# Two orders changed in a transformer trunk on one core: the spread of the row norms, and the keys of the memory attention

## The chip, the core and the metric

The kernel runs on one core of one Trainium2 chip. The core has five engines, each with its own in-order queue: TensorE (PE, matmul and weight load), VectorE (DVE), ScalarE (ACT), GpSimd (POOL) and SyncE (SP, which issues the DMAs here). They wait for each other through semaphores. The metric is the time of one execution on the device in microseconds (us), the median of several runs.

## What is computed

Two layers of a trunk over 512 tokens of width 1024, in float32. Cut to what the change touches:

```python
def _rmsnorm(x, g):
    y = xf * lax.rsqrt(jnp.mean(xf * xf, axis=-1, keepdims=True) + EPS)
    return y * g

for layer in range(2):
    x = x + 0.5 * _swiglu(_rmsnorm(x, ffn_pre_norm), w_gu, w_down)      # gate, up: 2816 each
    h = _rmsnorm(x, mix_norm)
    x = x + (_even_mixer(h, ...) if layer % 2 == 0 else _mla_mixer(h, ...))
    x = x + _memory_cross_attention(_rmsnorm(x, xmem_norm), _rmsnorm(mem, xmem_mem_norm), ...)
    x = x + 0.5 * _swiglu(_rmsnorm(x, ffn_post_norm), w_gu, w_down)

def _memory_cross_attention(hq, hm, wq, wkv, q_g, k_g, wo):              # 4 heads of 256, 256 memory tokens
    q = _rmsnorm((hq @ wq), q_g)
    k, v = jnp.split(hm @ wkv, 2)                                        # per head: 256 columns of k, 256 of v
    k = _rmsnorm(k, k_g)
    o = softmax(q @ k.T / 16) @ v
    return o @ wo
```

## The kernel before

The residual stream lies on chip with features on partitions (`x0` to `x7`, each 128 x 512 tokens). Every product runs as three passes (lines 98, 99 and 100) over operands split into a high and a low part: `hh` and `hl` for the activations, `wh` and `wl` for the weights. A weight granule (`gran`, 128 x 1024) is loaded by SP into `wr`, its high part is cast by ACT (line 79), and its low part is subtracted (line 83) by POOL, or by DVE where `lo="dve"` is given, as in the memory's products. Three raw buffers and four split ones stand between the loads and TensorE.

A norm's gain is put into `hh` and `hl`; its root mean square is applied to the product afterwards, so that the product needs no norm to begin. The factor comes in two steps, both in `stats`. First four short matmuls (line 147; the profile shows eight, since a float32 matmul is two) sum the squares `sqs` of each token, and a chain of small DVE operations (`rsqrt`, lines 106 to 114, and the copy to `rc`, line 151) takes the inverse root. If `bc` is set, DVE then builds four diagonal tiles `dg` (line 156), four matmuls spread them over all partitions (line 160), and ACT copies the result to `rbc` (line 162). `stats` with `bc` is called in each of the four FFNs after the first pair of products, and once in `sgu`, in layer 0's mixer, after the first chunk. The FFN multiplies `pg` (gate) and `pu` (up) by `rbc` on DVE (lines 220 and 222); its products take turns in five PSUM banks. In `sgu` the chunks are scaled by `rc`, and `rbc` is read much later, in `stick`.

`memkv` computes keys and values of the memory in eight chunks `c` of 256 columns: an even chunk is a head's key, the odd one after it its value. A key's chunk goes through ACT (`tk`, and its squares into `kss`), through the `rsqrt` chain on DVE and a multiplication by the result (line 928); then the closure `fin` turns it: four transposes on TensorE (line 935), ACT for the high part (line 939) and DVE for the low part (line 940). `fin` of a key is called after the next key's product, and that of the last key after the last value's product.

The code runs under a scheduler that sets each engine's order while the program is built, by a priority that follows the order of the code; nothing is reordered on the chip. `queued()` gives a rule to it: what the block issues on TensorE comes behind the last matmul that `self.pe` names (the last of a product).

Of the kernel before, what the change touches and what calls it, by code (L numbers as in the profile page):

```python
# [26 lines left out]
class Trunk:  # L27
    """The residual stream xT lives feature-major on chip; every product runs as
    three fp32r passes over operands split exactly into a high and a low part."""

    def __init__(self, ctx, tc, a, stop=None):
# [10 lines left out]
        # PSUM: two banks stay through all phases, which start in their own banks and end in these two,  # L42
        # so that no phase's first product waits for the last one's evacuation
# [3 lines left out]
    def queued(self):  # L47
        """What the block issues on the tensor engine comes behind what it had before."""
        return self.tc.issue_after(self.pe.ins)
# [9 lines left out]
    # ---------------------------------------------------------------- pieces  # L59
    def constants(self):  # L60
# [3 lines left out]
        # the first weights ahead of x: their split takes longer  # L64
# [10 lines left out]
    def split(self, hi, lo, src, eng_hi="act", eng_lo="dve"):  # L75
        """hi = src rounded to the multiplier's width, lo = src - hi (exact)."""
        nc = self.nc
        if eng_hi == "act":
            nc.scalar.copy(out=hi, in_=src)  # L79
        else:  # L80
            nc.vector.tensor_copy(out=hi, in_=src)
        e = nc.vector if eng_lo == "dve" else nc.gpsimd
        e.tensor_tensor(out=lo, in0=src, in1=hi.bitcast(F32), op=ALU.subtract)  # L83

    def gran(self, src, kt, cols, lo="pool"):
        """A weight granule [128, kt*cols] loaded and split."""
# [15 lines left out]
    def rsqrt(self, ssq, n, scale, eps, shape=None):  # L102
        """1/sqrt(ssq*scale + eps) on [128, n] by bit estimate and three Newton steps."""
# [13 lines left out]
    def prep(self, g, f):  # L117
        """Split gain*x_f for the next norm's consumers."""
# [12 lines left out]
    def squares(self, f):  # L131
        """Add the squares of x_f to the sums of the next norm."""
# [9 lines left out]
    def stats(self, pp, tag, bufs=None, bc=False):  # L142
        """rstd of every token: rc [128, NT] by token tile, and, if bc, rbc broadcast over partitions."""
# [10 lines left out]
        dg = self.t(self.sp, [P, NT, P], "dg", bufs=1)  # L154
        for t in range(NT):
            nc.vector.tensor_scalar(out=dg[:, t, :], in0=self.ident, scalar1=self.rc[:, t:t + 1], scalar2=None,
                                    op0=ALU.mult)
        ps = self.t(pp, [P, S], tag, bufs=bufs)
        for t in range(NT):
            nc.tensor.matmul(ps[:, t * P:(t + 1) * P], lhsT=self.ones, rhs=dg[:, t, :],  # L160
                             start=(t == 0), stop=(t == NT - 1), skip_group_check=True)
# [10 lines left out]
    def out_half(self, ps, w, src, kh, first):  # L172
        """One half of the contraction of a pair of out_proj's output tiles, in steps."""
# [7 lines left out]
    def out_proj(self, pp, tag, w, src, order, g, begun=None):  # L181
        """x += src @ w by pairs of output tiles; w in granules [pair*2 + khalf] of [128, 4, 256].
        begun: accumulators that hold the first half already."""
# [15 lines left out]
    # ---------------------------------------------------------------- FFN  # L199
    def ffn(self, w_gu, w_dn, g_next, out=None):  # L200
        nc, tc = self.nc, self.tc
        with tc.tile_pool(name=self.nm("ffn"), bufs=1) as fp, \
                tc.tile_pool(name=self.nm("ffps"), bufs=5, space=bass.MemoryType.PSUM) as pp:
            H = NFF // 2
            for half in range(2):
                acts = []
                for j in range(H):
# [8 lines left out]
                    if jj == 0:  # L216
                        self.stats(pp, "st", 1, True)
                    t1 = self.t(fp, [P, S], "t1", bufs=2)
                    t2 = self.t(fp, [P, S], "t2", bufs=2)
                    nc.vector.tensor_tensor(out=t1, in0=pg, in1=self.rbc, op=ALU.mult)  # L220
                    nc.scalar.activation(out=t1, in_=t1, func=AF.Silu)
                    nc.vector.tensor_tensor(out=t2, in0=pu, in1=self.rbc, op=ALU.mult)  # L222
                    nc.vector.tensor_tensor(out=t2, in0=t2, in1=t1, op=ALU.mult)
                    ah = self.t(fp, [P, S], f"ah{j}", F32R)
                    al = self.t(fp, [P, S], f"al{j}", F32R)
                    self.split(ah, al, t2, "act", "dve")
                    acts.append((ah, al))
# [15 lines left out]
    # ---------------------------------------------------------------- token-major products  # L243
    def tok_chunk(self, pp, tag, grans):
        """h @ w for 256 columns, token-major: two banks of [128, 2, 256]."""
# [11 lines left out]
    # ---------------------------------------------------------------- layer 0's mixer  # L257
# [15 lines left out]
    def sgu(self, p, pp, v, og):  # L273
# [8 lines left out]
        # only s <= t mixes: partition s, free t  # L282
# [12 lines left out]
        for dst, c0 in ((g, 0), (u, 2)):  # L295
            for c in range(2):
                ps = self.tok_chunk(pp, "mm", [w[(c0 + c) * 2], w[(c0 + c) * 2 + 1]])
                if first:
                    self.stats(pp, "tp", 2, True)
                    first = False  # L300
                for t in range(NT):
# [31 lines left out]
    def stick(self, p, pp, v, ob, src):  # L333
        """Stick-breaking attention, scores as [key, query]: causal blocks only."""
        nc, a = self.nc, self.a
        # key block -> (unit, column of its queries j*128.. in the unit); units are one bank each
# [9 lines left out]
        # -1 where row key >= column key  # L346
# [3 lines left out]
        # far below every score where key >= query: no softplus there, and no weight  # L350
# [10 lines left out]
        def proj(qk, pr, s):  # L361
            """q or k of a pair of heads, in steps."""
# [18 lines left out]
        def filler():  # L381
            """Products that wait for nothing, between the steps of the heads: the next pairs' q and k,
            and the part of the output projection that is fed by the gate."""
# [13 lines left out]
        def scores(h):  # L397
            """z of a head and the split softplus of its causal part."""
# [25 lines left out]
        def weights(st):  # L424
            """Suffix sums of the softplus, and the weights."""
# [41 lines left out]
    # ---------------------------------------------------------------- layer 1's mixer  # L467
    def rope_tables(self, p, op):
        """cos and sin of positions * inv_freq for [token, tile, 16], reduced modulo 2 pi by an
        exact digit scheme, and multiplied into the q and k gains of the two rope halves."""  # L470
# [59 lines left out]
    def mla(self):  # L530
        nc, tc, a = self.nc, self.tc, self.a
        H = 16
        with ExitStack() as outer:
# [20 lines left out]
            # the late tiles take the space of the stage before, so that the early ones need not wait for it  # L554
# [6 lines left out]
    def lora(self, p, pp, c, n, ss, cT, lg, j0):  # L561
        """rmsnorm of the token-major c [128, NT, n], turned feature-major and split."""
# [56 lines left out]
    def mla_attn(self, p, pl, pp, cT, krr, skr, gqk, neg, tq, o):  # L619
# [7 lines left out]
        def norms(st):  # L627
            """rstd of the heads' k (0) and q (1) from their sums of squares."""
            ss = st["ss"]
            # k's sums lack the rope part, which all heads share  # L630
# [11 lines left out]
        def proj_kv(st, g, t):  # L642
            """k (nope) and v of head group g, token tile t; after the last, the norms."""
# [22 lines left out]
        def proj_q(st, g, t):  # L666
            """q of head group g, token tile t; after the last, its rope."""
# [17 lines left out]
            # rope of q with its gains, in place  # L685
# [11 lines left out]
        def turn(st, h):  # L697
            """qT, kT [96, 512] of one head, split."""
# [17 lines left out]
        # query block -> (unit, column); key block j of the transposed weights likewise  # L716
# [4 lines left out]
        def filler():  # L721
            """The projections of the next head groups, a token tile at a time."""
# [18 lines left out]
        def scores(n, qk):  # L741
            """Scores of a head by query block, and their softmax."""
# [6 lines left out]
            for u, blks in enumerate(((3,), (2, 0), (1,))):  # L749
# [6 lines left out]
                # the last key block of every query block: side by side in the bank  # L756
# [24 lines left out]
        def weights(pb, wT, units):  # L781
            """The weights by key block."""
# [330 lines left out]
```

## Time and profile before

| | |
|---|---|
| median of 3 runs | 2326.71 us (2326.22 to 2329.08) |
| span of the profiled execution | 2328.0 us, 1.3 us over the median |
| TensorE busy | 98% of the span |
| VectorE, ScalarE, GpSimd busy | 44%, 38%, 39% |
| DMA | 209 MB, 29% of the 16 engines' time |

A busy share is an average over stages. The profile also lists, for each engine, whom it waited for and how long, and it can show the instructions of a stretch in order of time with the idle time of the engine before each. The granted clock is TensorE's: 1.00 is 2.4 GHz and 0.50 is 1.2 GHz. Time counts from the span's start. The ends of matmuls are modelled and overlap; how fast they follow each other is read from their starts.

### The profile page before, as it was taken

What the parts mean: (1) busy time and instruction counts of PE and PEld (TensorE: products, weight loads), DVE (VectorE), ACT (ScalarE), POOL (GpSimd) and SP (SyncE); (2) the same over time, 40 slices, a digit from 0 to 9 for tenths busy, and PEclk for the clock granted to TensorE, in tenths of its full rate; (3) what the DMA queues carried; (4) which work ended last, traced back from release to release, by engine and by line L of the source; (5) the groups of instructions that cost most, each with busy time, mean ns of one, the idle gap of its engine ahead of it and who ended that gap; (6) DMA issues with size and microseconds to landing.
All of it is one profiled execution on the core that took longest, in us unless ns stands there. A gap on an engine that the chain in (4) does not pass through costs nothing. (4 is left out here: it accounts for less than half of the span.)

```text
span 2328.0 us, 28369 instructions
## 1 busy us (share of the span) xinstructions
PE 2274.4 (98%) x11152; PEld 1891.5 (81%) x11152; DVE 1018.2 (44%) x1830; ACT 875.1 (38%) x1448; POOL 903.4 (39%) x441
## 2 busy tenths in 40 slices
PE   7999999999999999999999999998999999999999
PEld 6888888977988788888878888897768887888887
DVE  5322433465745533133343133368886545430330
ACT  4222233355644332232332223346655443322321
POOL 4444444201242444444544444434212323445443
PEclk9999999999999999999999999999999999999999
DMA  4223323311431232332322332321103313323322
GB/s 152 92 87 113 92 82 118 92 46 47 134 110 55 83 99 81 110 100 83 108 90 83 108 100 86 99 80 57 37 19 119 127 55 91 91 79 111 100 81 92
DMA packets 67350, 208.65 MB, mean 90 GB/s; under 512 B 8592, under 2 KB 10640, under 8 KB 67216
## 3 DMA queue, kind: packets, MB, share of 16 engines
q1 hardware_dynamic: 67216, 206.83, 29.1%
q8 instruction: 88, 1.44, 0.3%
q14 instruction: 46, 0.38, 0.1%
HBM read 204.70 MB, written 2.10 MB: 89 GB/s over the span
## 5 line engine op out<-in xcount | busy, mean ns | idle before, releaser
L83 POOL TENSOR_TENSOR wl<-wr,wh 128x1024 fp32r<-128x1024 f32 (+2 forms) x382 | 850.6, 2227 | 1253.0 <-ACT wh L79 1188.8
L79 ACT CAST wh<-wr 128x1024 fp32r<-128x1024 f32 (+3 forms) x423 | 408.7, 966 | 1029.8 <-PE mm L99 540.7
L98 PE MATMUL mm<-hh,wh 128*128 128x512 f32 x1440 | 562.8, 391 | 6.6 <-ACT hh L125 6.6
L100 PE MATMUL mm<-hh,wl 128*128 128x512 f32 x1440 | 562.5, 391 | 0.9 <-POOL wl L83 0.9
L99 PE MATMUL mm<-hl,wh 128*128 128x512 f32 x1440 | 562.2, 390 | 0.5 <-DVE hl L126 0.5
L98 PEld LDWEIGHTS mm<-hh,wh 128*128 128x128 f32 x1440 | 271.5, 189 | 62.9 <-ACT hh L125 6.6
L100 PEld LDWEIGHTS mm<-hh,wl 128*128 128x128 f32 x1440 | 271.6, 189 | 57.6 <-POOL wl L83 1.3
L99 PEld LDWEIGHTS mm<-hl,wh 128*128 128x128 f32 x1440 | 271.3, 188 | 57.6 <-DVE hl L126 1.0
L98 PE MATMUL A<-ah,wh 128*128 128x512 f32 x704 | 277.4, 394 | 0.0
L100 PE MATMUL A<-ah,wl 128*128 128x512 f32 x704 | 276.0, 392 | 0.0
L99 PE MATMUL A<-al,wh 128*128 128x512 f32 x704 | 273.2, 388 | 0.0
L222 DVE TENSOR_TENSOR t<-mm,rbc 128x512 f32<-128x512 f32 x88 | 60.8, 691 | 390.5 <-PE mm L100 390.5
L234 DVE SCALAR_TENSOR_TENSOR x<-A,x 128x512 f32<-128x512 f32 x64 | 44.3, 691 | 354.3 <-PE A L100 354.3
L83 DVE TENSOR_TENSOR al<-t,ah 128x512 fp32r<-128x512 f32 x88 | 160.8, 1828 | 59.1 <-ACT ah L79 59.1
L100 PEld LDWEIGHTS A<-ah,wl 128*128 128x128 f32 x704 | 132.1, 188 | 31.0
L99 PEld LDWEIGHTS A<-al,wh 128*128 128x128 f32 x704 | 132.2, 188 | 29.6
L98 PEld LDWEIGHTS A<-ah,wh 128*128 128x128 f32 x704 | 132.3, 188 | 26.4
L220 DVE TENSOR_TENSOR t<-mm,rbc 128x512 f32<-128x512 f32 x88 | 60.9, 692 | 117.1 <-PE mm L100 110.8
L126 DVE SCALAR_TENSOR_TENSOR hl<-x,gc,hh 128x512 fp32r<-128x512 f32 x64 | 82.8, 1307 | 36.7 <-ACT hh L125 36.6
L98 PE MATMUL A<-hh,wh 128*128 128x512 f32 x224 | 91.6, 410 | 0.7 <-ACT hh L79 0.7
L99 PE MATMUL A<-hl,wh 128*128 128x512 f32 x224 | 90.0, 402 | 0.0
L100 PE MATMUL A<-hh,wl 128*128 128x512 f32 x224 | 89.8, 401 | 0.0
(322 smaller groups left out, 3260.6 us busy)
## 6 DMA issues: line engine op xcount, KB each, us to landing
wr<-in_w_gu SPq DMA_DIRECT2D x176, 512.0 KB, 3.6
wr<-in_w_dn SPq DMA_DIRECT2D x64, 384.0 KB, 3.1
wr<-in_w_dn SPq DMA_DIRECT2D x64, 320.0 KB, 2.9
wr<-in_xmem_wkv SPq DMA_DIRECT2D x32, 512.0 KB, 3.2
wr<-in_xmem_wq SPq DMA_DIRECT2D x16, 512.0 KB, 3.3
wr<-in_xmem_wo SPq DMA_DIRECT2D x16, 512.0 KB, 3.2
wr<-in_sbg_w_zv SPq DMA_DIRECT2D x12, 512.0 KB, 3.5
wr<-in_sbg_w_qk SPq DMA_DIRECT2D x8, 512.0 KB, 3.6
```

The source lines that it names most:

```text
L79: nc.scalar.copy(out=hi, in_=src)
L83: e.tensor_tensor(out=lo, in0=src, in1=hi.bitcast(F32), op=ALU.subtract)
L98: mm(out, lhsT=A[0], rhs=B[0], start=start, stop=False, skip_group_check=True)
L99: mm(out, lhsT=A[0], rhs=B[1], start=False, stop=False, skip_group_check=True)
L100: self.pe = mm(out, lhsT=A[1], rhs=B[0], start=False, stop=stop, skip_group_check=True)
L126: nc.vector.scalar_tensor_tensor(out=hl, in0=self.x[f], scalar=col, in1=hh.bitcast(F32), op0=ALU.mult, op1=ALU.subtract)
L220: nc.vector.tensor_tensor(out=t1, in0=pg, in1=self.rbc, op=ALU.mult)
L222: nc.vector.tensor_tensor(out=t2, in0=pu, in1=self.rbc, op=ALU.mult)
L234: nc.vector.scalar_tensor_tensor(out=self.x[m], in0=ps, scalar=0.5, in1=self.x[m], op0=ALU.mult, op1=ALU.add)
```

## The change

Three things are altered, and comments are taken out.

- `stats` ends with the diagonal tiles, and the four spreading matmuls with the copy to `rbc` become a function of their own, `spread`.
- In `ffn` the sums are issued right behind one product and the spread right behind the next one: behind the first and the second product in three FFNs, behind the second and the third in the first FFN of the program (`s0` is 1 there). There the gating of the first pair is written behind the second pair. In `sgu` the spread is issued behind the third chunk instead of in the second.
- In `memkv` the chunks come in the order 0, 2, 1, 4, 3, 6, 5, 7, and a key is turned when two more chunks have been issued.

```diff
     def stats(self, pp, tag, bufs=None, bc=False):
@@
-        dg = self.t(self.sp, [P, NT, P], "dg", bufs=1)
+        self.dg = self.t(self.sp, [P, NT, P], "dg", bufs=1)
         for t in range(NT):
-            nc.vector.tensor_scalar(out=dg[:, t, :], in0=self.ident, scalar1=self.rc[:, t:t + 1], scalar2=None,
+            nc.vector.tensor_scalar(out=self.dg[:, t, :], in0=self.ident, scalar1=self.rc[:, t:t + 1], scalar2=None,
                                     op0=ALU.mult)
+
+    def spread(self, pp, tag, bufs=None):
+
+        nc, dg = self.nc, self.dg
         ps = self.t(pp, [P, S], tag, bufs=bufs)
         for t in range(NT):
-            nc.tensor.matmul(ps[:, t * P:(t + 1) * P], lhsT=self.ones, rhs=dg[:, t, :],
-                             start=(t == 0), stop=(t == NT - 1), skip_group_check=True)
+            self.pe = nc.tensor.matmul(ps[:, t * P:(t + 1) * P], lhsT=self.ones, rhs=dg[:, t, :],
+                                       start=(t == 0), stop=(t == NT - 1), skip_group_check=True)
         nc.scalar.copy(out=self.rbc, in_=ps)
@@ ffn: gated() holds the lines that stood in the loop (t1, t2, ah, al)
+            s0 = 1 if self.first else 0
+            todo = []
...
-                    if jj == 0:
-                        self.stats(pp, "st", 1, True)
...
+                        n = 2 * jj + (ps is pu)
+                        if n in (s0, s0 + 1):
+                            with self.queued():
+                                self.stats(pp, "st", 1, True) if n == s0 else self.spread(pp, "st", 1)
+                    todo.append((j, pg, pu))
+                    if 2 * jj > s0 or s0 == 0:
+                        for z in todo:
+                            acts.append(gated(*z))
+                        todo = []
@@ sgu
                 if first:
                     self.stats(pp, "tp", 2, True)
                     first = False
+                elif dst is u and c == 0:
+                    with self.queued():
+                        self.spread(pp, "tp", 2)
@@ memkv
-        fin = None
-        for c in range(8):
+        fins = []
+
+        for n, c in enumerate((0, 2, 1, 4, 3, 6, 5, 7)):
...
+            while fins and fins[0][0] <= n - 2:
+                with self.queued():
+                    fins.pop(0)[1]()
             if c % 2 == 1:
...
-                if c == 7:
-                    fin()
                 continue
-            if fin is not None:
-                fin()
...
+            fins.append((n, fin))
```

TensorE's queue at the start of the second FFN, before: `mm_6537` is the second product (`pu` of the first pair), `mm_6640` the third; each has 24 matmuls.

```order
L100 MATMUL mm_6537<-hh_1144_6517,wl_6571 128x512
L147 MATMUL st_6598<-ones_105,sqs_6288 128x1 x4
L98 MATMUL mm_6640<-hh_1100_6279,wh_6644 128x512
...
L98 MATMUL mm_6640<-hh_1116_6361,wh_6644 128x512
L99 MATMUL mm_6640<-hl_1117_6362,wh_6644 128x512
L160 MATMUL st_6624<-dg_6619,ones_105 128x128 x4
L100 MATMUL mm_6640<-hh_1116_6361,wl_6645 128x512
L98 MATMUL mm_6640<-hh_1128_6434,wh_6644 128x512
```

The same place in the changed program; `mm_6536` is the first product.

```order
L100 MATMUL mm_6536<-hh_1144_6517,wl_6541 128x512
L147 MATMUL st_6568<-ones_105,sqs_6288 128x1 x4
L98 MATMUL mm_6537<-hh_1100_6279,wh_6596 128x512
...
L98 MATMUL mm_6537<-hh_1144_6517,wh_6596 128x512
L99 MATMUL mm_6537<-hl_1145_6518,wh_6596 128x512
L100 MATMUL mm_6537<-hh_1144_6517,wl_6597 128x512
L164 MATMUL st_6624<-dg_6589,ones_105 128x128 x4
L98 MATMUL mm_6640<-hh_1100_6279,wh_6644 128x512
```

The sums (`st` with `sqs`) moved one product earlier, and between them and the spread (`st` with `dg`) now stand 24 matmuls instead of 11.

TensorE's queue at the end of `memkv` in layer 0, before: `mm_5328` is the last key's chunk (`tk_5399` is made from it), `mm_5422` the last value's, of 48 matmuls each, and `A_5508` the first product of the queries.

```order
L100 MATMUL mm_5328<-wh_5361,ml_854_4813 128x256
L935 MATMUL at_5389<-ident_100,tk_5239 128x128 x2
L935 MATMUL at_5394<-ident_100,tk_5239 128x128 x2
L98 MATMUL mm_5422<-wh_5425,mh_832_4757 128x256
...
L100 MATMUL mm_5422<-wh_5455,ml_854_4813 128x256
L935 MATMUL at_5488<-ident_100,tk_5399 128x128 x2
L935 MATMUL at_5493<-ident_100,tk_5399 128x128 x2
L98 MATMUL A_5508<-hh_742_4482,wh_5511 128x512
```

The same place in the changed program: `mm_5262` is the last key's chunk (`tk_5333` is made from it), `mm_5356` and `mm_5422` are the last two values'.

```order
L100 MATMUL mm_5262<-wh_5295,ml_854_4813 128x256
L956 MATMUL at_5323<-ident_100,tk_5173 128x128 x2
L956 MATMUL at_5328<-ident_100,tk_5173 128x128 x2
L98 MATMUL mm_5356<-wh_5359,mh_832_4757 128x256
...
L100 MATMUL mm_5422<-wh_5455,ml_854_4813 128x256
L956 MATMUL at_5483<-ident_100,tk_5333 128x128 x2
L956 MATMUL at_5488<-ident_100,tk_5333 128x128 x2
L98 MATMUL A_5508<-hh_742_4482,wh_5511 128x512
```

Between the last key's chunk and its transposes now stand two chunks (96 matmuls) instead of one. SP's queue is the same in both programs.

## Rows read from the trace of the kernel before

**Rows 1.** Page, part 1: busy time, share of the span, instructions.

```profile
PE 2274.4 (98%) x11152; PEld 1891.5 (81%) x11152; DVE 1018.2 (44%) x1830; ACT 875.1 (38%) x1448; POOL 903.4 (39%) x441
```

**Rows 2.** TensorE's waits: for whom, us in total, times, longest.

```profile
PE st L160 <- DVE dg L156: 8.8, 4, 2.4
PE at L935 <- DVE tk L928: 7.8, 2, 3.9
...
PE A L98 <- ACT prk L657: 3.0, 1, 3.0
...
PE tp L160 <- DVE dg L156: 2.6, 1, 2.6
```

**Rows 3.** TensorE by stretch: length, busy, instructions, granted clock, DMA share, GB/s.

```profile
397.90:401.30 3.40, 3.40 (x18) 0.50 0.02 5
804.00:807.50 3.50, 3.02 (x11) 0.51 0.25 101
1170.50:1174.00 3.50, 3.21 (x18) 1.00 0.19 76
664.00:670.90 6.90, 5.86 (x16) 0.51 0.17 67
1834.90:1841.70 6.80, 5.71 (x16) 0.50 0.20 72
```

**Rows 4.** Timeline, last FFN: start, us, engine, line, tiles, idle before, releaser.

```profile
1963.15 0.68 DVE L140 TENSOR_TENSOR sqs<-sqs,sq 128x512 f32<-128x512 f32 x1
...
1964.62 0.39 PE L98 MATMUL mm<-hh,wh 128*128 128x512 f32 x1
...
1970.06 0.95 PE L147 MATMUL st<-ones,sqs 128*128 128x1 f32 x8
...
1970.87 0.49 PE L98 MATMUL mm<-hh,wh 128*128 128x512 f32 x1
...
1971.20 2.41 POOL L83 TENSOR_TENSOR wl<-wr,wh 128x1024 fp32r<-128x1024 f32 x1 [3.05 <-ACT wh L79]
1971.24 2.40 DVE L108 TENSOR_SCALAR rs_y<-rs_v 128x4 int32<-128x4 int32 x1
...
1976.08 1.13 PE L160 MATMUL st<-dg,ones 128*128 128x128 f32 x8 [2.41 <-DVE dg L156]
```

**Rows 5.** Timeline of TensorE in `sgu`, behind the spread.

```profile
398.04 0.56 PE L98 MATMUL mm<-wh,hh 128*128 128x256 f32 x1
...
401.36 0.28 PE L98 MATMUL mm<-wh,hh 128*128 128x256 f32 x1
401.48 0.28 PE L99 MATMUL mm<-wl,hh 128*128 128x256 f32 x1
```

**Rows 6.** Timeline of TensorE in layer 0's `memkv`.

```profile
643.00 0.60 PE L935 MATMUL at<-ident,tk 128*128 128x128 f32 x4
...
654.83 0.60 PE L935 MATMUL at<-ident,tk 128*128 128x128 f32 x4
...
660.85 0.28 PE L100 MATMUL mm<-wh,ml 128*128 128x256 f32 x1
665.04 1.09 PE L935 MATMUL at<-ident,tk 128*128 128x128 f32 x4 [3.91 <-DVE tk L928]
```

**Rows 7.** Timeline of VectorE and GpSimd in the same stage.

```profile
650.46 0.62 DVE L928 TENSOR_SCALAR tk<-tk,rs_y 128x256 f32<-128x256 f32 x2
651.33 1.22 DVE L83 TENSOR_TENSOR wl<-wr,wh 128x1024 fp32r<-128x1024 f32 x1
...
658.38 2.06 DVE L106 TENSOR_SCALAR rs_v<-kss 128x2 f32<-128x2 f32 x1 [1.59 <-ACT kscr L925]
660.47 2.27 DVE L108 TENSOR_SCALAR rs_y<-rs_v 128x2 int32<-128x2 int32 x1
...
664.54 0.61 DVE L928 TENSOR_SCALAR tk<-tk,rs_y 128x256 f32<-128x256 f32 x2
...
658.01 4.71 POOL L83 TENSOR_TENSOR wl<-wr,wh 128x1024 fp32r<-128x1024 f32 x2 [1.97 <-ACT wh L79]
```

More of the change, by code (lines that the diff above doesn't have):

```diff
@@ L204, in ffn, with gated @@
             H = NFF // 2
+            s0 = 1 if self.first else 0
+            todo = []
+            def gated(j, pg, pu):
+                t1 = self.t(fp, [P, S], "t1", bufs=2)
+                t2 = self.t(fp, [P, S], "t2", bufs=2)
+                nc.vector.tensor_tensor(out=t1, in0=pg, in1=self.rbc, op=ALU.mult)
+                nc.scalar.activation(out=t1, in_=t1, func=AF.Silu)
+                nc.vector.tensor_tensor(out=t2, in0=pu, in1=self.rbc, op=ALU.mult)
+                nc.vector.tensor_tensor(out=t2, in0=t2, in1=t1, op=ALU.mult)
+                ah = self.t(fp, [P, S], f"ah{j}", F32R)
+                al = self.t(fp, [P, S], f"al{j}", F32R)
+                self.split(ah, al, t2, "act", "dve")
+                return ah, al
             for half in range(2):
@@ L215, in ffn @@
                             self.mm3(ps, (wh[:, k, :], wl[:, k, :]), (self.hh[k], self.hl[k]), k == 0, k == KT - 1)
-                    if jj == 0:
-                        self.stats(pp, "st", 1, True)
[L218 to L227, printed above, removed]
+                        n = 2 * jj + (ps is pu)
[7 more added lines that the diff above has]
+                        todo = []
                 for m in range(KT):
```

## The prediction

> **What bounds the kernel now.** I read the page's busy times first: TensorE works 98% of the span and no other engine half of it [rows 1]. The matmuls are the same before and after, so the change can only win TensorE's idle time and whatever the idle time costs behind itself. So I read TensorE's waits next. Three of their groups belong to the lines that the change touches: the spreads of the four FFNs wait for the diagonal tiles, 8.8 us in all and at most 2.4 each; the spread in `sgu` waits 2.6; the last key's transposes in `memkv` wait for `tk`, 3.9 in each of two layers [rows 2]. Together 19.2 us, in seven places. The third view is the granted clock around these places. Behind the wait in `sgu` it was 0.50 for 3.4 us; in one FFN it was about 0.51 over 3.5 us, while the same place in the next FFN kept 1.00; behind both `memkv` waits it was 0.50 to 0.51 for nearly 7 us [rows 3]. So a wait can cost more than itself: behind four of the seven a stretch at 1.2 instead of 2.4 GHz follows, behind others none.
>
> **What the waits cost, part by part.** The listed idle time counts from the modelled end of a matmul. By starts, the last key's transposes begin 4.19 us after the matmul before them [rows 6], where the next start would come 0.12 later [rows 5]: 4.07 lost and not 3.91. The difference of some 0.16 in each of seven places adds 1.1, so that the idle part is 19.2 + 1.1 = 20.3 us.
>
> The clock's part: in `sgu`, 16 matmuls lie between 398.04 and 401.36, and at full clock one follows another in 0.12 [rows 5], so 3.32 - 1.92 = 1.4 lost. In the FFN, equal stretches of 3.5 us hold 11 instructions at half clock and 18 at full [rows 3]; a matmul of 512 columns takes 0.227 (24 of them from 1964.62 to 1970.06 [rows 4]), so 7 x 0.227 = 1.6 lost. In `memkv` the half clock lasts from 665.04 [rows 6] to about 670.9 and holds 16 instructions [rows 3], four transposes and twelve matmuls: 5.9 less 12 x 0.227 = 2.7 and less at most 0.6 for transposes that met no wait [rows 6], so 2.6 lost, and as much in the other layer, whose stretch is as long. Sum 1.4 + 1.6 + 2 x 2.6 = 8.2 us.
> The Trainium skill (TensorE: Matmul & The Clock Gate, Terms) puts the penalty of a throttled stretch at its length times one less the granted share. By that the four stretches of rows 3, about 20.6 us together, would be worth 10.3, and the sum below 2.1 us better. I take the rows, since part of a stretch is filled by the short matmuls, which lose less.
>
> **Does the cover suffice?** In three FFNs the spread now stands 13 matmuls later than it did, 24 instead of 11 behind the sums. 13 x 0.227 = 2.95 us of work against 2.6 of lateness (2.41 idle and the 0.16): hidden with 0.35 to spare, thin, but the two sides run in step. The chain takes 6.0 us from the sums at 1970.06 to the spread at 1976.08, and 2.40 of it is one step, `rs_y`, that began 0.04 after GpSimd's split of a granule and ended with it [rows 4]. The split is released by TensorE's products, so one product earlier the chain should meet the split of that product at the same point. The sums must also be ready one product earlier: the squares ended at 1963.15 + 0.68 = 1963.83, and the first product ended at 1964.62 [rows 4], 0.8 to spare. The first FFN's wait, 8.8 - 3 x 2.41 = 1.6, is covered by the same 2.95; its gating comes a product later, and its four products still leave the fifth PSUM bank for the next. In `sgu` the spread moves behind the third chunk, over 170 matmuls of 0.12 us on, against a chain that was 2.6 late; `rbc` is read only in `stick`. The four spreading matmuls, their copy and the tiles are neither more nor fewer: zero.
>
> In `memkv` a key chunk's `tk` was ready 8.1 us after its transposes' neighbour at 643.00 (650.46 + 0.62), and for the last key 10.3 us after 654.83 (664.54 + 0.61), since there GpSimd's splits for the queries held two small steps for 2.06 and 2.27 [rows 6, 7]. Before, one chunk stood between, 6.1 us from 654.83 to 661.0 with the transposes. Now two do, and such a stretch is shown: 643.00 to 654.83, 11.8 us [rows 6]. So even the slow chain has 1.5 us to spare and the quick one 3.7. The first two keys now come one behind the other, so that the second chain waits for the first: 8.1 plus the steps of one more chain, 2.4 by rows 4 (1973.64 to 1976.08), is 10.5 of 11.8. DVE also splits the weights in this queue, and the last split of the stage began at 651.33, done 2.6 us before the last value's chunk began at all [rows 7, 6], so a split that comes two or three us later still comes in time. SP's loads stand in the same order.
>
> **The sum.** 20.3 + 8.2 = 28.5 us if all seven waits go and no half clock comes in their place. Some may: waits remain, such as 3.0 us in the second layer's mixer, which kept the full clock here [rows 2], and which wait is followed by half clock differs from place to place [rows 3]. I take one of 1.5 every second time, 0.7, and 0.4 for thin covers. That leaves 27.4. The profiled span is 2328.0, so 2300.6 by it; it stood 1.3 over the median, so the forecast is 2326.7 - 27.4 = 2299.3 us.
>
> **The rivals.**
> The chain is held twice. `memkv` shows two of its steps held one after the other [rows 7]. If the chains in their new places meet a second split, 2.3 us more each: three FFNs lose 2.3 - 0.35 = 1.95 each, the two last keys 2.3 - 1.5 = 0.8 each, 7.5 in all, and two stretches of half clock at 1.5 follow: 2299.3 + 10.5 = 2309.8. For it, the FFN's margin is small; against it, GpSimd splits one granule per product there, 2.4 of 5.4 us, and the one step that it held went on when the split ended [rows 4]. Chance 0.10.
> The Trainium skill (SBUF — State Buffer, Who interferes with whom) says that GpSimd and VectorE share a pair of ports as an exclusive lock, held for a whole instruction, and that the loser is blocked fully; 2.40 beside 2.41 in rows 4 agrees, and by that rule alone every further split that a chain meets would give this rival's time.
>
> The half clock stays. If TensorE falls to 1.2 GHz at the remaining waits as often as it did here, only the idle part is won: 2326.7 - 20.3 = 2306.4. For it: a fall does not follow every wait, so another place can take its turn. Against it: the waits that remain are mostly shorter. Chance 0.07.
>
> The change does nothing: the idle time reappears at the next join (the gating, the queries' norms), 2326.7, or 2322 at best. Against it: TensorE does not read `rbc` or the turned keys until several products later. Chance 0.03.
>
> Slower: weights starved in `memkv`. DVE does the weights' low parts and the key chains in one queue. If all four keys' chains of a layer were held as the last one was, 4.0 us each (2.06 + 2.27 less two of 0.16), and the splits behind them came that late without the slack of rows 7, TensorE would lose 16 us a layer and 32 in both, 3.5 more than is won: 2330. It decides from 3.6 us a key on. Against it: GpSimd has next to nothing to split in this stage before its end. Chance 0.04, with what I do not see.
>
> **How the numbers follow.** Forecast 0.76. The range must reach to 2310.5 to take in both partial cases; its lower end is the full sum, 2326.7 - 28.5 = 2298.2, less 3 us for what the sum may hold too little (two more stretches of half clock at 1.5, behind waits that stay, that happen not to come): 2295. That leaves about 1 in 10 out. A measurement of this kernel can tell 0.2%, 4.7 us, from no change. Faster 0.76 + 0.10 + 0.07 = 0.93, the same 0.03, slower 0.04.
>
> **What would show it.** TensorE's waits no longer list a spread for `dg` over 0.3 us nor transposes for `tk` over 0.5; the stretches of half clock behind them are gone, and four fewer are seen in all, or three. A wait of the FFN spreads of about 2 us, with two steps of the chain held, would show the first rival; half clock in layer 1's mixer the second; TensorE waiting for `wl` in `memkv` the last. The prediction is wrong if TensorE's idle time falls by less than 17 us.

## The result, and the profile after

The changed kernel takes 2301.9 us (median; 2301.2 to 2303.64), the one before 2327.89 beside it: a ratio of 0.9886, 95% interval 0.9872 to 0.99. The forecast was 2299.3 with a range of 2295.0 to 2310.5, so 27.4 us were expected and 26.0 came. (The forecast counted from 2326.71, the kernel before as measured until then.) The profiled span is 2301.9 against 2328.0: 26.1 less.

The first line of the page after, to be read against [rows 1]: engine, busy time, share, instructions.

```profile
PE 2267.7 (99%) x11152; PEld 1887.0 (82%) x11152; DVE 1020.5 (44%) x1830; ACT 875.1 (38%) x1448; POOL 902.7 (39%) x441
```

It splits the 26.1. TensorE's busy time fell by 2274.4 - 2267.7 = 6.7 with the same 11152 instructions, so they ran faster: that is, in the main, the clock's part. The rest, 26.1 - 6.7 = 19.4, is idle time that is gone. The forecast's split, 7.5 and 19.9, counts by starts. There some 1.1 of the 6.7 belong to the idle part, since the last matmul before each of the seven waits counts as busy 0.16 us beyond its usual distance: 5.6 and 20.5.

TensorE's waits after (for whom, us in total, times, longest), the lines that answer to [rows 2] and the largest others that are spoken of below:

```profile
PE A L98 <- ACT prk L678: 3.0, 1, 3.0
PE z L454 <- DVE tl L83: 3.0, 3, 1.0
PE st L147 <- DVE sqs L140: 2.7, 1, 2.7
...
PE st L164 <- DVE dg L156: 0.2, 1, 0.2
```

Of the seven waits, 19.2 us, one of 0.2 is left (the first FFN's spread); the transposes for `tk` and the spread in `sgu` are not listed at all. What remains was there before and is no part of the change: the mixer of layer 1 for `prk`, the stick attention for `tl`, the kernel's first sums for `sqs`.

How the last FFN looks now, beside [rows 4] (start, length, engine, line, operation, tiles; in brackets idle time before and the releaser):

```profile
1941.25 0.95 PE L147 MATMUL st<-ones,sqs 128*128 128x1 f32 x8
...
1942.38 2.41 POOL L83 TENSOR_TENSOR wl<-wr,wh 128x1024 fp32r<-128x1024 f32 x1 [3.08 <-ACT wh L79]
1942.43 2.39 DVE L108 TENSOR_SCALAR rs_y<-rs_v 128x4 int32<-128x4 int32 x1
...
1946.83 0.87 DVE L156 TENSOR_SCALAR dg<-ident,rc 128x128 f32<-128x128 f32 x4
...
1947.64 1.05 PE L164 MATMUL st<-dg,ones 128*128 128x128 f32 x8
...
1948.78 2.40 POOL L83 TENSOR_TENSOR wl<-wr,wh 128x1024 fp32r<-128x1024 f32 x1 [3.98 <-ACT wh L79]
```

The chain still meets one split of GpSimd at the same point (2.39 beside 2.41), as the prediction had it. The spread begins 6.39 us behind the sums with no wait. The diagonal tiles are done at 1947.70, 1.08 before GpSimd's next split: that distance becomes important below.

TensorE, VectorE and GpSimd in layer 0's `memkv`, the place of [rows 6, 7], the last key's chain between its neighbours' transposes and its own:

```profile
645.54 0.60 PE L956 MATMUL at<-ident,tk 128*128 128x128 f32 x4
...
650.15 2.40 POOL L83 TENSOR_TENSOR wl<-wr,wh 128x1024 fp32r<-128x1024 f32 x1 [5.74 <-ACT wh L79]
650.22 2.34 DVE L112 TENSOR_TENSOR rs_u<-rs_y 128x2 f32<-128x2 f32 x1
...
654.16 0.61 DVE L949 TENSOR_SCALAR tk<-tk,rs_y 128x256 f32<-128x256 f32 x2
...
657.37 0.60 PE L956 MATMUL at<-ident,tk 128*128 128x128 f32 x4
```

The transposes now stand 657.37 - 645.54 = 11.83 us apart, the stretch that was forecast as 11.8; `tk` is ready at 654.77, so 2.6 us are to spare. This chain was held once and not twice as in [rows 7].

**The granted clock.** In this profile there is half clock (a granted clock of 0.50) behind none of the changed places; two stretches of it stand at other places. The changed kernel by stretch (length; busy time and instructions of PE, PEld, DVE, ACT, POOL; granted clock of TensorE, DMA share, GB/s):

```profile
505.63:512.40 6.77, 6.77 (x16) 4.46 (x15) 4.97 (x12) 4.26 (x9) 0.00 (x0) 0.51 0.01 2
...
1560.20:1563.60 3.40, 3.40 (x10) 2.82 (x10) 0.63 (x2) 1.38 (x6) 0.00 (x0) 0.50 0.00 0
```

and the same work in the kernel before:

```profile
512.34:516.08 3.74, 3.74 (x18) 2.55 (x16) 2.04 (x6) 3.46 (x8) 0.00 (x0) 1.00 0.02 4
...
1577.30:1580.70 3.40, 3.40 (x17) 3.12 (x18) 1.48 (x5) 2.46 (x7) 0.00 (x0) 1.00 0.00 1
```

The first pair is a stretch of the attention in layer 0 (`stick`) from the same score matmul to the same `av`: 6.77 us at 1.2 GHz against 3.74 at 2.4, so 3.03 lost. (The Trainium skill, TensorE: Matmul & The Clock Gate, Terms, puts the penalty at length times one less the share, an estimate of 6.77 x 0.49 = 3.3 beside the 3.03 measured: long matmuls fill nearly all of this stretch, and the rule comes close.) The second pair is the mixer behind its wait for `prk`: 10 instructions where 17 went before, 7 x 0.227 = 1.6 lost. Both waits, 1.00 for `tl` and 3.0 for `prk`, are equally long in both kernels. The one before had the full clock behind them, the changed one has not. That the first pair belongs to the wait for `tl` is read from its place alone: TensorE goes on at 503.03, and the half clock begins 2.4 us later.

By the starts of TensorE's matmuls, place by place (what lies between two starts beyond the usual distance):

| place | before, us lost | after |
|---|---|---|
| first FFN: spread, and half clock ahead of it | 3.3 | 0.4 |
| FFN 1, 2, 3: spread and behind it | 4.1, 2.8, 2.8 | 0, 0, 0 |
| `sgu`: spread and behind it | 4.4 | 0 |
| `memkv`, layers 0 and 1 | 6.8, 6.7 | 0, 0 |
| stick attention, the stretch above | 0 | 3.0 |
| layer 1's mixer, behind `prk` | 0 | 1.6 |
| sum | 30.9 | 5.0 |

30.9 - 5.0 = 25.9, the change of the span within 0.2. Of the 30.9, 10.0 stand in half clock (1.6 in the first FFN, 1.5 in FFN 1, 1.6 in `sgu`, 2.7 and 2.6 in `memkv`) and 20.9 in waits; of the 5.0, 4.6 and 0.4. By starts the change is thus 5.4 of clock and 20.5 of idle time.

The first FFN needs a closer look. Before, its sums wait 2.6 us for the squares, which the change doesn't touch, and half clock follows, ahead of the spread:

```profile
24.64 1.05 PE L147 MATMUL st<-ones,sqs 128*128 128x1 f32 x8 [2.61 <-DVE sqs L140]
...
31.46 1.13 PE L160 MATMUL st<-dg,ones 128*128 128x128 f32 x8 [1.55 <-DVE dg L156]
```

```profile
25.80:29.20 3.40, 3.40 (x9) 2.65 (x9) 3.30 (x4) 0.00 (x0) 3.33 (x2) 0.50 0.67 211
```

The spread begins 31.46 - 24.64 = 6.82 us behind the sums. In `e4_filled_wait` (below), whose FFNs are those of the kernel before, TensorE has the full clock from the sums to the end of its work ahead of the spread; there the spread begins 6.84 us behind the sums (24.91 and 31.75) and waits 3.14 instead of 1.55. The chain sets this time, so before the change half clock ahead of the spread cost nothing of its own. After it the spread hardly waits, and half clock there costs. The profile above has none; of the twelve profiles here in which these sums wait, it is the only one without half clock in the first FFN. From the start of the sums to one and the same matmul of the fourth product TensorE took 12.6 us before (24.64 to 37.24), 9.7 in the profile above (25.07 to 34.74), and 10.8 in two further profiles of the changed kernel, `e0` and `e12` below, that have half clock there.

### The profile page after: what moved, and what is told of

It is laid out like the page before. It is cut to its first block, busy times and chain, and to the rows that moved or that the text cites. A ratio compares the mean times of both kernels' runs of the same rounds, so it can differ in the third digit from the quotient of the medians.

```text
span 2301.9 us, 28372 instructions
## 1 busy us (share of the span) xinstructions
PE 2267.7 (99%) x11152; PEld 1887.0 (82%) x11152; DVE 1020.5 (44%) x1830; ACT 875.1 (38%) x1448; POOL 902.7 (39%) x441
```

## The experiments

Each group of four runs shared a chip and its runs of the kernel before; these took 2329.93, 2328.61 and 2327.38 us (medians of 15, 21 and 7 runs).

### The three parts, one at a time

`e0_after_again` is the changed kernel again.

> The changed kernel once more, for its own spread and for a second trace. Theory (idle time gone, and the half clock is a matter of chance at whatever waits remain): 25 to 27 us less than before, again without a wait of a spread or of a key's transposes; the half clock stands in other places than in the first trace of it (which had 6.8 us in layer 0's attention and 3.4 in layer 1's mixer), or in one of them. Rival (the half clock is made by the new order itself): the same two places, of the same lengths.

Measured: 2301.3 us, ratio 0.9879 (0.9865 to 0.9892), 28.6 less than before on this chip, where 25 to 27 were expected; the kernel before took 2.0 us longer here than beside the first result. The waits are those above. Half clock stands in this profile for 3.4 us at the first FFN and 3.4 in layer 1's mixer, none in the `stick` attention: the place differs from one execution to the next.

`e1_ffn_alone` has the new `stats`, `spread` and `ffn`; `memkv` is as before, and `sgu` spreads at once:

```diff
                 self.stats(pp, "tp", 2, True)
+                self.spread(pp, "tp", 2)
```

> The FFN's part alone (sums behind one product, spread behind the next), with the mixer's spread and the keys as before. Theory: the four waits go, 1.7 + 3 x 2.6 = 9.4 us, and the half clock behind them, 1.6 on average at most: 9 to 11 us less than before. Rival (the parts hang together, and the time comes mostly from the keys): under 5.

Measured: 2318.31 us, ratio 0.9946 (0.9933 to 0.996), 11.6 less. Its waits:

```profile
PE at L955 <- DVE tk L948: 7.8, 2, 3.9
...
PE tp L164 <- DVE dg L156: 2.4, 1, 2.4
```

`e2_keys_alone` is the kernel before with the new `memkv`:

```diff
-        for c in range(8):
+        for n, c in enumerate((0, 2, 1, 4, 3, 6, 5, 7)):
...
+            while fins and fins[0][0] <= n - 2:
```

> The keys' part alone (order 0, 2, 1, 4, 3, 6, 5, 7, turned two chunks on). Theory: both waits of 4.07 go and the half clock of nearly 7 us behind each, worth 2.6: 13 us less than before, 11 if one more stretch of half clock falls elsewhere. Rival (only the idle time is won, the half clock comes with the queries' products anyway): 8.

Measured: 2315.59 us, ratio 0.9944 (0.9931 to 0.9956), 14.3 less. Its waits:

```profile
PE st L160 <- DVE dg L156: 9.4, 4, 2.4
...
PE tp L160 <- DVE dg L156: 3.3, 1, 3.3
```

`e3_sgu_alone` has the new `stats`, `spread` and `sgu`; the FFN spreads at once:

```diff
                         self.stats(pp, "st", 1, True)
+                        self.spread(pp, "st", 1)
```

> The spread in layer 0's mixer alone, behind the third chunk. Theory: the wait of 2.7 goes, and the half clock behind it where it falls, 1.4: 2.7 to 4.1 us less than before. Rival (the norm's chain is still in the way, since the chunk's scaling waits for it too): no change.

Measured: 2325.21 us, ratio 0.9978 (0.9969 to 0.9987), 4.7 less. Its waits:

```profile
PE at L943 <- DVE tk L936: 7.8, 2, 3.9
PE st L164 <- DVE dg L156: 7.6, 4, 2.4
```

What follows: each part takes away its own waits and leaves the others much as they were (the FFNs' 8.8 became 9.4 in e2 and 7.6 in e3). The granted clock agrees: e1 has no half clock behind the spreads of its three later FFNs, e2 none in `memkv`, e3 none in `sgu`, while e1 and e3 keep it behind both `memkv` waits. By the prediction's terms the three were worth 8.8 + 4 x 0.16 + 1.6 = 11.0, 7.8 + 2 x 0.16 + 5.2 = 13.3 and 2.6 + 0.16 + 1.4 = 4.2; measured were 11.6, 14.3 and 4.7, each a little over what was expected. They add up to 30.6, and the whole gave 28.6 on the same chip. Each interval is some 2 to 3 us wide to either side, so this difference of 2 isn't told from none.

### Idle time and clock told apart

`e4_filled_wait` leaves the last key late and gives TensorE useless work meanwhile:

```diff
                 if c == 7:
-                    fin()
+                    pf = self.psA()
+                    with self.queued():
+                        for i in range(14):
+                            self.pe = nc.tensor.matmul(pf, lhsT=self.hh[0][:, 0:P], rhs=self.hh[1], ...)
+                    with self.queued():
+                        fin()
```

> The kernel before, with 14 matmuls of 512 columns into a spare PSUM bank queued ahead of the last key's transposes in memkv, so that TensorE works through most of the 3.9 us for which it waited (14 x 0.227 = 3.2 us). It adds work that nobody needs. Theory (a wait costs twice: the idle time itself, and half clock behind it): the idle time is only filled, so it wins nothing, but the half clock behind the two waits goes, 2 x 2.6 = 5 us less than before: ratio 0.998. The listed wait for tk falls from 3.9 to about 0.7 a layer and no stretch of half clock starts near 664 or 1835. Rival (the half clock there does not hang on the wait): the stretches stay, and the time is that of before: ratio 1.000.

Measured: 2325.88 us, ratio 0.9987 (0.9978 to 0.9996): 2.7 less than before (0.9 to 5.1 by the interval), though it does more work. The place in layer 0, to be read beside [rows 6]:

```profile
663.70 3.36 PE L919 MATMUL A<-hh,hh 128*128 128x512 f32 x14
667.82 0.50 PE L941 MATMUL at<-ident,tk 128*128 128x128 f32 x2 [0.77 <-DVE tk L934]
```

The transposes come as late as before, 667.82 - 663.57 = 4.25 behind the value's last matmul (4.19 in rows 6), so nothing of the idle time is won. The clock in this kernel, behind the two filled waits and at three other places:

```profile
663.00:671.00 8.00, 7.23 (x38) 5.83 (x37) 6.21 (x15) 2.62 (x5) 5.15 (x4) 1.00 0.41 134
1833.00:1842.00 9.00, 8.23 (x44) 6.77 (x43) 7.21 (x15) 2.62 (x5) 6.15 (x4) 1.00 0.36 117
1170.90:1174.30 3.40, 3.23 (x12) 2.98 (x13) 1.14 (x5) 0.59 (x1) 0.00 (x0) 0.50 0.16 64
1976.40:1979.80 3.40, 3.40 (x10) 2.63 (x9) 1.29 (x2) 2.46 (x3) 0.00 (x0) 0.50 0.00 0
1580.50:1583.90 3.40, 3.40 (x13) 3.29 (x12) 1.94 (x4) 1.65 (x4) 1.28 (x1) 0.50 0.02 5
```

So the theory holds: the half clock in `memkv` hung on the wait. The filled wait kept 1.00 in both layers, where the profiles of before, e1 and e3 have half clock behind both waits. But of the 5 us that this should be worth only 2.7 stayed. The last three lines show where the rest went in this execution, the slowest of the eleven (2330.4): two FFNs and layer 1's mixer ran at 0.50 behind waits that were there before too, and the first FFN did so for 6.8 us. The first of these FFNs had 1.00 there in [rows 3], the mixer in the row of before above.

### How much room the chain has

`e6_long_chain` and `e9_five_steps` are the changed kernel with a longer chain between sums and spread, seven and five Newton steps (rounds of three operations in `rsqrt`) instead of three. The edit of e6; e9 has `steps=5`:

```diff
-        y = self.rsqrt(ps[:, 0:NT], NT, 1.0 / D, EPS)
+        y = self.rsqrt(ps[:, 0:NT], NT, 1.0 / D, EPS, steps=7 if bc else 3)
```

> The changed kernel with seven instead of three Newton steps in the chain between the sums and the spread (FFNs and sgu): 12 more small operations on VectorE, some 2.4 us. Theory (the FFN cover of 2.95 us exceeds the lateness of 2.6 by 0.35 only): TensorE waits for dg again at the spread, about 2.0 us in each of three FFNs and about 1.2 in the first, none in sgu, 7 us more than the changed kernel, up to 10 with half clock behind some of them: ratio to before 0.991 to 0.992. Rival (the chain has more room in its new place than I worked out, since one step is no longer held): waits below 0.5 each and a time within 2 us of the changed kernel's, ratio 0.988.

Measured: 2324.78 us, ratio 0.998 (0.9971 to 0.9988). Against `e8_sums_one_later_all` beside it, which costs what the changed kernel does, that is 24.7 us more, where 7 to 10 were expected. TensorE's wait line and the timeline of the last FFN show why:

```profile
PE st L164 <- DVE dg L156: 11.9, 3, 4.0
```

```profile
1953.01 2.41 POOL L83 TENSOR_TENSOR wl<-wr,wh 128x1024 fp32r<-128x1024 f32 x1 [3.08 <-ACT wh L79]
1953.05 2.39 DVE L108 TENSOR_SCALAR rs_y<-rs_v 128x4 int32<-128x4 int32 x1
...
1959.40 2.34 POOL L83 TENSOR_TENSOR wl<-wr,wh 128x1024 fp32r<-128x1024 f32 x1 [3.98 <-ACT wh L79]
1959.42 2.34 DVE L114 SCALAR_TENSOR_TENSOR rs_y<-rs_u,rs_y 128x4 f32<-128x4 f32 x1
...
1962.43 1.63 PE L164 MATMUL st<-dg,ones 128*128 128x128 f32 x8 [4.01 <-DVE dg L156]
```

Twelve steps of 0.2 made the chain 2.4 longer, and its last step then began 0.02 behind GpSimd's next split and ended with it: 2.34 for an operation of 0.16. (The Trainium skill, SBUF — State Buffer, Who interferes with whom, has GpSimd and VectorE share a port pair as an exclusive lock; both holds here, 2.39 beside a split of 2.41 and 2.34 beside one of 2.34, agree with it.) So the spreads wait 4.0 and not 2.0 in three FFNs, some 6 us more than expected. A stretch of 3.4 us at 0.50 follows each of the three, and another stands in the mixer: 4 x 1.6 = 6.4. With 11.9 that is 18.3 of the 20.1 that the profiled execution lies over e8's median; the timed runs lie up to 6 us higher still at a lower mean clock, which I put down to more half clock without having their profiles.

> The changed kernel with five instead of three Newton steps in the chain between the sums and the spread, six more small operations on VectorE, 6 x 0.2 = 1.2 us, half of what the run with seven steps added. Theory (the cover of the FFNs has 0.4 us to spare, and the chain is held a second time only if it reaches GpSimd's next split, 1.1 us behind its end): the spread waits about 0.8 us in each of three FFNs and about 1.4 in the first, 3 to 4 us more than the changed kernel and no half clock behind them; ratio to before 0.989 to 0.990. Rival (the last step of the chain meets the next split already): waits of 3 us and half clock behind them, 10 us more or worse, ratio 0.992 to 0.998.

Measured: 2305.52 us, ratio 0.9896 (0.9877 to 0.9914), 4.7 more than the changed kernel beside it (2300.79). Its wait line, and the last FFN:

```profile
PE st L164 <- DVE dg L156: 1.9, 3, 0.6
```

```profile
1950.02 0.88 DVE L156 TENSOR_SCALAR dg<-ident,rc 128x128 f32<-128x128 f32 x4
1950.42 0.97 PEld L164 LDWEIGHTS st<-dg,ones 128*128 128x128 f32 x8 [1.03 <-PE mm L100]
1950.45 1.13 PE L164 MATMUL st<-dg,ones 128*128 128x128 f32 x8 [0.64 <-DVE dg L156]
1950.78 2.38 POOL L83 TENSOR_TENSOR wl<-wr,wh 128x1024 fp32r<-128x1024 f32 x1 [3.99 <-ACT wh L79]
```

By starts the spread comes 0.80 late in each of three FFNs, as expected; the split begins when the last diagonal tile is under way, and nothing is held. The first FFN has no wait, against the 1.4 expected: it ran at half clock there, which stretches the cover. In this profile the half clock at the first FFN and in the mixer lasts 6.8 us each, where the changed kernel's on the same chip lasts 3.4: 2.4 + 2 x 1.6 = 5.6, about the 4.7 to 5.5 measured.

The two together give the margin: 0.4 us free, then 0.6 per added Newton step at each of three FFNs, and past the next split of GpSimd another 2.2 at each, with half clock behind each in e6's profile.

### The place of the sums

`e8_sums_one_later_all`:

```diff
-            s0 = 1 if self.first else 0
+            s0 = 1
```

> The changed kernel with the sums of the three later FFNs behind the second product and their spread behind the third, as the first FFN has it; the cover between the two is the same product. Theory (what hides the chain is the product between sums and spread, not the place of the sums): no wait of the spread for dg over 0.5 us, and the changed kernel's time within 2 us: ratio 0.987 to 0.989. Rival (in the new place the chain meets a second split of GpSimd and is held for 2.3 us more, or the gating of two tiles at once makes a later product wait for PSUM): waits of about 2 us in three FFNs, 6 us more: ratio 0.990 to 0.991.

Measured: 2300.06 us, ratio 0.988 (0.9866 to 0.9893), no wait of the spread listed. In these two places it is the distance between sums and spread that counts, and not where the pair stands.

### The waits that the change left

`e7_sums_later` moves the first FFN's sums, which wait 2.7 us for the squares, one product further; `e10_two_squares` gives the mixer's `prk` a second buffer; `e11_both` does both.

```diff
-            s0 = 1 if self.first else 0
+            s0 = 2 if self.first else 0
...
-                    if 2 * jj > s0 or s0 == 0:
+                    if 2 * jj + 1 >= s0 + 1:
```

```diff
-            s2 = self.t(p, [P, G, 64], "prk", bufs=1)
+            s2 = self.t(p, [P, G, 64], "prk", bufs=2)
```

> The changed kernel with the sums of the first FFN alone issued one product later still, and the spread with them; the cover between sums and spread stays one product. Theory (the 2.7 us for which the sums wait for the squares at the kernel's start is a wait of its own, with half clock behind it in some runs): that wait goes and nothing takes its place, 2.7 us less than the changed kernel, 4.3 with the half clock: 2297 to 2299 where the changed kernel takes 2301.3, ratio to before 0.986 to 0.987. Rival (the products behind wait for the same input rows anyway, or the gating that comes a product later takes the time back): the wait of 2.7 shows at another line and the time is the changed kernel's, ratio 0.988.

Measured: 2297.67 us, ratio 0.9869 (0.9854 to 0.9884), 2.4 less than e8 beside it, as expected, though the intervals (some 3.5 us to either side) would not tell that by itself. The wait for `sqs` is no longer listed and none took its place. Half clock stands only in the mixer, and now 6.8 us long:

```profile
1552.80:1559.60 6.80, 5.91 (x16) 5.33 (x17) 3.47 (x9) 2.91 (x8) 1.22 (x1) 0.50 0.14 51
```

> The changed kernel with two buffers instead of one for the squares of the keys in layer 1's mixer (prk), so that ScalarE need not wait for VectorE's sum of the ones before. Theory (the 3.0 us wait there, which the change left, is a single buffer's, and the half clock behind it is that wait's): the wait falls under 0.7 us, and no stretch of half clock starts near 1555 to 1560: 2.3 us of idle time and, as often as the stretch was there, 1.5 to 3 us more: 2.3 to 5 us less than the changed kernel, ratio to before 0.986 to 0.987. Rival (the wait only moves to the next use of the two accumulators, because VectorE's queue is what is late): a wait of 2 us or more stands at another line of the mixer, and the time is the changed kernel's, ratio 0.988.

Measured: 2298.98 us, ratio 0.987 (0.9852 to 0.9889), 1.8 less than the changed kernel beside it; 2.3 to 5 were expected, and the intervals don't tell 1.8 from none. The wait fell to 1.6 only, not below 0.7, and part of the expected gain is missing for that: ScalarE still waits 1.9 us for VectorE's sum of an earlier square. No half clock follows it.

> The changed kernel with both: the first FFN's sums one product later, and two buffers for the squares of the keys. The two waits of about 3 us that the change left, and behind which half clock was seen after it, are both gone. Theory (each win is its own wait and the half clock behind it, so they add): 3.4 + 3 to 5 = 6 to 8 us less than the changed kernel, 2293 to 2296 where it takes 2301.5, ratio to before 0.984 to 0.986, and the granted clock's mean above 0.999. Rival (half clock takes another wait, as those in the attentions): one or two stretches of it at other places, 2296 to 2299, ratio 0.986 to 0.988.

Measured: 2294.93 us (2294.85 to 2298.43), ratio 0.9854 (0.9835 to 0.9874): 5.9 less than the changed kernel, and 4.05 less than e10, which differs by the first FFN alone: 2.7 is its wait, and the rest, some 1.4, I put down to the clock. Its four runs and the changed kernel's four (2300.16 to 2301.84) don't overlap. The waits of e11, and its mean granted clock:

```profile
PE z L454 <- DVE tl L83: 3.0, 3, 1.0
PE A L98 <- ACT prk L678: 1.6, 1, 1.6
```

```profile
core 0: 2293.2 us, clock 1.000
```

The only half clock left in its trace stands at the kernel's end, behind TensorE's work. This is the fastest of all. The rival, that half clock takes other waits instead, did not come about in the profiled execution; the slowest run, 2298.43 at a mean clock of 0.999, lies in the rival's range and has no profile.

> The changed kernel unaltered, beside the three others on their chip. 2301 to 2302, ratio 0.988; the waits of its first profile; stretches of half clock, if any, at the kernel's first sums and in layer 1's mixer, the two places where a wait of 2.7 to 3.0 us is left.

Measured: 2300.79 us, ratio 0.9876 (0.9854 to 0.9898), with 3.4 us of half clock at the first FFN and 3.4 in the mixer, as in e0.

Put side by side, half clock at three waits that the change left, in single profiles of the kernel before and of kernels that hold the whole change (us of it; a dash where there is none):

| place and its wait | before | after | e0, e12 | e8 | e7 | e10 | e11 |
|---|---|---|---|---|---|---|---|
| first sums, 2.7 (gone in e7, e11) | 3.4 | - | 3.4 | 6.8 | - | 3.4 | - |
| `stick` attention, 1.0 | - | 6.8 | - | - | - | - | - |
| mixer, 3.0 (1.6 in e10, e11) | - | 3.4 | 3.4 | - | 6.8 | - | - |

## Why the prediction was right

**What bounds the kernel.** Right. Only TensorE's idle time and the clock changed; its busy instructions are the same.

**The idle part, 20.3.** Right: the waits fell from 19.2 to 0.2, and 20.5 was won by starts, 19.4 by the page's line, where less than 17 would have refuted it. Each part alone (e1 to e3) takes away its own waits, so the three parts are separate.

**The clock's part, 8.2.** The mechanism is right and shown apart from the idle time by e4. The four stretches lost 1.5 + 1.6 + 2.7 + 2.6 = 8.4 by starts. A fifth, 1.6 ahead of the first FFN's spread, the sum didn't see, because I looked only behind the seven waits. Before, it cost nothing of its own, but it hid half of that spread's wait. With half clock there, as in e0 and e12, the change wins 12.6 - 10.8 = 1.8 in the first FFN, which is the sum's 1.6 + 0.16; the profile after won 2.9, and the 1.1 more is luck.

**The covers.** The FFN's 0.35 to spare was right: 0.38 in the trace after (the tiles would have let the spread begin at 1946.83 + 0.43 = 1947.26; it began at 1947.64), and e9's 0.80 for 1.2 more agrees. That sums and splits move in step was right as well. `memkv` had 2.6 to spare where 1.5 was worked out, since only one step was held and not two.

**What comes back, 1.1.** This is the step that failed. I took one stretch of 1.5 every second time, 0.7, and 0.4 for covers. In the profile after, the covers cost the 0.4, but 3.0 and 1.6 came back as half clock, 4.6 instead of 0.7. Against the 28.5 of the sum, 30.9 went and 5.0 came back instead of 1.1: two errors of 2.4 and 3.9 us that mostly cancel, the first in part by the luck in the first FFN. That the forecast came within some 1.4 of the gain is owed to this. The place in the mixer was named beforehand, as one that could take its turn; the `stick` attention, with its wait of 1.0, was not. That waits with the full clock behind them in one profile may have half clock in the next could have been read from rows 3, where one FFN fell and its equal did not.

**The rivals.** Chain held twice: not in the changed kernel, but it is real, and 1.08 us away, as e6 shows; in e6 half clock followed each of the three waits, where I had priced two stretches in all; what the second hold costs the unaltered chain no run shows. Half clock stays: partly. Five stretches stood in the profile before and two in the one after, one of them in layer 1's mixer, the rival's sign, and 4.6 us came back where the rival has all 8.2 stay. Nothing: no. Weights starved: no wait for a `wl` of VectorE is listed.

**What stays open.** Which of two equal waits is followed by half clock isn't settled by these runs, nor whether half clock comes back because other waits went. In the mixer, behind its 3.0 us, it stands in two of five profiles without the whole change (e1, e4) and in six of seven with it (not in e8): that hints at it and doesn't show it. The other timed runs have no profiles, only mean clocks: 0.993 to 0.996 in all 43 runs of the kernel before on the three chips, 0.998 to 0.999 in all 12 of the changed one, and 1.000 in three of four of e11.

## What to carry to other kernels

Where the busiest engine waits for a chain of small steps on another, put one more independent piece of its work between the two ends of the chain, and count the room left to the next long instruction that can hold the chain, not only to the wait. Price such a wait as idle time plus the half clock behind it, but expect half clock at some of the waits that stay; in e11, where two of those were removed or halved, it was gone from TensorE's work in the profile, and the mean clock was 1.000 in three of four runs. Half clock ahead of a join that waits for another engine cost nothing here, until the wait was covered. Busy time at an equal number of instructions tells idle time and clock apart in one line of the page, here to about 1 us.

## What the runs showed of the hardware

A wait of 1.00 us in the `stick` attention, equally long in both kernels, had 1.00 of the clock behind it before and 0.51 over 6.77 us after. The 3.0 us in layer 1's mixer had the full clock behind them in four profiles (before, e2, e3, e8) and half clock for 3.4 or 6.8 us in the other eight where the wait was that long. A wait that was filled with 14 useless matmuls (3.36 us) kept the full clock behind it in both layers and made the kernel 2.7 us faster (0.9 to 5.1) than leaving TensorE idle. A VectorE operation on 128 x 4 elements took 0.16 us alone and 2.34 when it began 0.02 behind a GpSimd split of 2.34.
